# Shifted tile addresses in a three-pass float32 transformer step: gated tiles at three residues, features at a fourth

## The chip, the cores and the metric

The kernel runs on one core of one Trainium2 chip (trn2). The metric is the device time of one execution in microseconds (us); three runs of the kernel before gave a median of 757.47 us, the lowest 757.41 and the highest 758.09. The trace comes from one further execution that took 756.95 us, of which 755.2 us lie between the first and the last instruction (the span). Engines are named as in the profile: PE is the matmul engine, PEld its weight loads, DVE, ACT and POOL the vector, activation and general engines, SP the queue that issues most transfers.

## The reference

One layer of a diffusion backbone over 512 latent tokens and 128 context tokens, 640 in all, width 1024, everything in float32:

```python
h = _rms(x, norm_mix) * (1 + sc1) + sh1          # modulated features
proj = h @ w_in                                  # q, k, v, gb, gc, u
attn = _block_attention(q_r, k_all, v_all)
y_conv = gb * _short_conv(gc * u, conv_w)
merged = jnp.concatenate([_rms(attn, ...), _rms(y_conv, ...)], axis=-1)
x = x + g1 * (merged @ w_out)
h2 = _rms(x, norm_ffn) * (1 + sc2) + sh2
gate, up = jnp.split(h2 @ w_gate_up, 2, axis=-1)
x = x + g2 * ((jax.nn.silu(gate) * up) @ w_down)
```

The context tokens go through the same layer with their own modulation. Nothing in the change touches what is computed.

## The kernel before

**Splits.** A float32 operand is held as two tiles of the type float32r, a rounded high part and the remainder. `split` (lines 150 to 152) makes them: ACT copies the high part, DVE subtracts it. A product is then three matmuls, `mm3` (lines 154 to 157): high by high, high by low, low by high. In `pe.matmul(out, lhsT, rhs)` the second argument is loaded into the array as weights (128 columns of 4 bytes, 512 bytes in each partition) and the third streams past it (the moving operand, 256, 320 or 512 columns). The weight load of a matmul is issued while the matmul ahead of it streams, so at any moment PE reads two places of a partition: the moving operand of one matmul and the weights of the next.

**Which tiles meet.** `wh` and `wl` are the splits of a weight matrix and live in pool A for the whole program. What they meet, in order of time:

- q and k/v: features `hH`, `hL` (modulated, normed x) are loaded, `wh`, `wl` stream: 512 columns for q, 256 for k and v.
- the convolution branch, `conv_mm` (lines 703 to 716), in pieces between the steps of the attention: `wh`, `wl` are loaded, `hH`, `hL` stream with 320 columns.
- the attention itself: KA, KB, VS, qT, ph, pl, none of them beside `wh`.
- the output projection: the mixed features `mx` are loaded (for the last latent block `sx`, for the attention half of the context `m0`, printed as `m` by the profile), `wh`, `wl` of w_out stream with 512 columns.
- gate and up: a scheme with seven products on halves; operands made from w_gate_up are loaded from `wh`, `wl`; the token halves B11, B12, B21, B22 and their sums T1 to T4 stream with 320 columns.
- down: the gated features `gT` (silu(gate) times up, split) are loaded, `wh`, `wl` of w_down stream with 512 columns (256 in the last part). Groups of six, six, five and five of 22 feature blocks; two blocks share one `gT` tile.

**Addresses.** Tiles are placed by pools that are stacked from the left and the right end of each partition, so the size of an early tile shifts all later ones on its side. Two tiles that nothing reads serve for that: `placeA` at the end of pool A on the left (line 601) and `placeF` first on the right (line 170), of PLACE = 48 and 72 floats, 192 and 288 bytes. Slices that are loaded start at whole multiples of 512 bytes in their tile, and moving slices at multiples of 256, so a tile's address modulo 512 tells that of its slices up to 256.

**The ring of gated tiles.** The tag `gT` has GB = 3 buffers of 10,240 bytes in pool GT. It first holds the two tiles of `h2` (line 985), then B12 (line 1045, in `b_tile`), then the gated pairs (line 1183, in `ff_out`). A new tile takes the buffer that the scheduler finds free first.

**Order.** PE runs in program order throughout (`manual_schedule`), and so does DVE around the first products of the feed-forward part; elsewhere the tile layer orders ACT and DVE by priority.

Of the kernel before, what the change touches and what calls it, by code (L numbers as in the profile page):

```python
# [9 lines left out]
F32 = mybir.dt.float32  # L10
F32R = mybir.dt.float32r
# [4 lines left out]
P = 128  # L16
# [4 lines left out]
TOK = NT * P  # L21
# [7 lines left out]
HALF = TOK // 2  # L29
# [21 lines left out]
GB = 3  # L51
# [29 lines left out]
QTB = 3  # L81
WFB = 3
WHB = 4
PLACE = 48, 72
AHEAD = 3
OSQ = 2
AFB = 4
# [4 lines left out]
def build(ctx, tc, x_prompt, x_sample, c, cache_k, cache_v, c_ctx, norm_mix, norm_ffn, w_ada, b_ada,  # L92
# [8 lines left out]
    def open_pool(name, side, names):  # L101
        g = tc.tile_pool(name=name, bufs=1, side=side, reuse_waits="tile")
        pools[name] = (g, g.__enter__())
        for n in names.split():
            where[n] = name
# [7 lines left out]
    def close_pool(name):  # L113
        pools[name][0].__exit__(None, None, None)
# [5 lines left out]
    def T(tag, shape, dt=F32, bufs=1):  # L120
        seq[0] += 1
        return pools[where.get(tag, "A")][1].tile(list(shape), dt, tag=tag, bufs=bufs, name=f"{tag}_{seq[0]}")

    def PB(shape=(P, 512), dt=F32, tag="t"):
        seq[0] += 1
        if kept.get(tag):
            w = kept[tag].pop()
            n = 1
            for y in shape[1:]:
                n *= y  # L130
            w = w[:, :n] if tag != "s" else w
            if tag != "s" and len(shape) > 2:
                names = "abc"[:len(shape) - 1]
                w = w.rearrange("p (" + " ".join(names) + ") -> p " + " ".join(names), **dict(zip(names, shape[1:])))
            return w
        return pools["psum"][1].tile(list(shape), dt, tag=tag, bufs=pbufs[tag], name=f"p{tag}_{seq[0]}")
# [4 lines left out]
    def T2(shape, dt=F32):  # L141
        return T("t2", shape, dt, 2)
# [4 lines left out]
    def early(n):  # L147
        return tc.high_priority(n)

    def split(hi, lo, src):  # L150
        act.activation(hi, src, AF.Copy)  # L151
        dve.tensor_tensor(lo, src, f32(hi), ALU.subtract)  # L152
# [6 lines left out]
    def rstd_of(ss, n, scale, by=1.0, tag="rs"):  # L159

        w = ss.shape[1]
        ms = T("ms", (P, w), F32, 4)
        dve.tensor_scalar(ms, ss, scale * by, EPS * by, ALU.mult, ALU.add)
        r = T(tag, (P, w), F32, {"rB": 1, "rs": 6}.get(tag, NT))
        pool.tensor_tensor(r, ms, neghalf[:, :w], ALU.pow)
        return r

    open_pool("A", "left", "")
    open_pool("F", "right", "placeF of y oz ysum m0 g1 rs5 cp")
    T("placeF", (P, PLACE[1]))  # L170
    open_pool("H", "right", " ".join(f"hH{k} hL{k}" for k in range(KD)))
# [428 lines left out]
    close_pool("B0")  # L600
    T("placeA", (P, PLACE[0]))
    open_pool("B2", "left", "vt KA KB VS qT pr ph pl osq c25 aw es")
# [359 lines left out]
    for x in SEQ.split():  # L962
        if "." in x:
            n, i = (int(y) for y in x[1:].split("."))
# [11 lines left out]
        for _ in range(1):  # L976
            kept[x] = [PS2() if x == "s" else PB(tag=x)]
    open_pool("X", "left", "x2 x2n g2 sx")
    open_pool("GT", "left", "gT")
    open_pool("Y1", "left", "B11 B21")  # L980
    open_pool("D", "right", "mix mx aacc bb")
    phase[0] = 2


    h2 = [T("gT", (P, 4, TOK), F32, GB) for _ in range(2)]
    LO, HI = slice(0, HALF), slice(HALF, TOK)
    x2 = [None] * NT
    x2n = {}
# [53 lines left out]
    B = {}  # L1042

    def b_tile(name):
        w = T("gT" if name == "B12" else name, (P, 2, 4, HALF), F32R, GB if name == "B12" else 1)
        B[name] = [(w[:, 0, i], w[:, 1, i]) for i in range(4)] + [w]

    def quarter(name, part):
# [3 lines left out]
    def b_put(name, src, part):  # L1052
        if name not in B:
            b_tile(name)
        w = B[name][4]
        if name in BHD:
            dve.tensor_copy(w[:, 0, :, part], src)
        else:
            act.activation(w[:, 0, :, part], src, AF.Copy)
        dve.tensor_tensor(w[:, 1, :, part], src, f32(w[:, 0, :, part]), ALU.subtract)  # L1060
# [17 lines left out]
    for j in range(2):  # L1078
        cols = slice(j * 512, (j + 1) * 512)
        for n, t in enumerate(TORD):  # L1080
# [33 lines left out]
            with early(XP[j]):  # L1114
                m = T("mix", (P, 512), F32, 2)
# [6 lines left out]
                else:  # L1122
# [3 lines left out]
                    m = T("mix", (P, 512), F32, 2)  # L1126
# [25 lines left out]
    gT, st, pair = {}, {}, [None]  # L1152
# [9 lines left out]
    def plain(f, bs, toks, mid=None):  # L1162

        ps = [FB(), FB()]
        for x, a in zip(ps, ("A1", "A2")):
            for i in (1, 2):
                if mid is not None and (a, i) == ("A2", 2):
                    mid()
                prod(x, f, f"{a}{i}", bs[i - 1], i == 1, i == 2)
        if toks is LO:  # L1170
            st[f] = T("cg", (P, TOK), F32, 2), T("cu", (P, TOK), F32, 2)
        cg, cu = st[f]
        act.activation(cg[:, toks], ps[0][:, :HALF], AF.Silu)
        dve.tensor_tensor(cu[:, toks], ps[1][:, :HALF], cg[:, toks], ALU.mult)
        if toks is HI:
            ff_out(f, cu)
            del st[f]

    def ff_out(f, cu):
        grp = next(g for g in GROUPS if f in g)  # L1180
        i = (f - grp[0]) % 2
        if i == 0:
            pair[0] = T("gT", (P, 2, 2, TOK), F32R, GB)
        gT[f] = (pair[0][:, i, 0], pair[0][:, i, 1])
        with early(GSP):
            split(gT[f][0], gT[f][1], cu)
# [41 lines left out]
    def ff_end(f):  # L1228
        cg, cu, b3, u2 = st.pop(f)
        dve.tensor_tensor(cg[:, HI], b3[:, :HALF], u2, ALU.add)  # L1230
        act.activation(cg[:, HI], cg[:, HI], AF.Silu)
        dve.tensor_tensor(cu[:, HI], cu[:, HI], cg[:, HI], ALU.mult)
        ff_out(f, cu)
# [78 lines left out]


tile_hymba = with_exitstack(build)

_INS = ["x_prompt", "x_sample", "c", "cache_k", "cache_v", "c_ctx", "norm_mix", "norm_ffn", "w_ada", "b_ada",
# [44 lines left out]
```

## Time and profile before

| what | value |
|---|---|
| median of three runs | 757.47 us |
| profiled execution, whole | 756.95 us |
| its span | 755.2 us |
| PE busy in the span | 737.5 us, 4618 matmuls |
| DVE, ACT, POOL busy | 551.7, 378.8, 42.6 us |
| granted PE clock, mean | 0.999 |

In the rows of a view an instruction stands with its engine, its line, its operation, the tile written and those read, the shape, how many, the busy time and the mean of one in ns. For a matmul "ph<-wh,mx" names the output and both inputs, not which of them moves. Matmuls are pipelined: one of 512 columns is listed with some 389 ns, yet the next starts some 227 ns after it, so the cost of a matmul in a row of them is read from the starts, not from the duration.

### The profile page before, as it was taken

How to read it: one execution, taken by the hardware profiler on the slowest of the kernel's cores; microseconds unless marked ns; L12 is line 12 of the kernel's file. 1: busy time of each engine (PE TensorE's matmuls, PEld its weight loads, DVE VectorE, ACT ScalarE, POOL GpSimd, SP SyncE). 2: the span in 40 equal slices, each digit the busy share in tenths (PEclk: the TensorE clock that was granted, in tenths of full speed). 3: DMA queues.
4: the chain of work that ended last, by engine and by line, in shares of the span. 5: the costliest groups of instructions: out<-in, count | busy, mean ns of one | idle time of the engine just before them, and what ended most of it. 6: DMA issues, size and time to landing. Idle time of an engine off the chain costs nothing.

```text
span 755.2 us, 11953 instructions
## 1 busy us (share of the span) xinstructions
PE 737.5 (98%) x4618; PEld 665.2 (88%) x4618; DVE 551.7 (73%) x997; ACT 378.8 (50%) x745; POOL 42.6 (6%) x75
## 2 busy tenths in 40 slices
PE   7999899999999999999999999999999999999997
PEld 5678888988998887899998799998889998899986
DVE  5558877666666798779979778884678866788653
ACT  5356777667656534765552235553125541255410
POOL 2403101011000110100000000000000000000000
PEclk9999999999999999999999999999999999999999
DMA  9985133532432464031235313133113232222312
GB/s 290 294 236 163 51 104 102 165 92 91 159 107 91 133 224 138 1 112 54 81 118 157 108 58 110 58 111 112 56 56 104 67 112 78 62 86 84 112 56 83
DMA packets 101389, 84.52 MB, mean 112 GB/s; under 512 B 3502, under 2 KB 81650, under 8 KB 101332
## 3 DMA queue, kind: packets, MB, share of 16 engines
q1 hardware_dynamic: 100980, 83.39, 35.9%
q8 instruction: 36, 0.59, 0.3%
q0 software_dynamic: 352, 0.37, 0.3%
q14 instruction: 21, 0.17, 0.1%
HBM read 79.68 MB, written 2.75 MB: 109 GB/s over the span
## 4 chain that ended last, share of the span: by engine, by line
PE 83%; DVE 7%; ACT 5%; DMA 2%; issue 1%; SPq 1%; POOL 0%; ACTq 0%
PE pf L155 17%; PE pf L157 17%; PE pf L156 17%; PE pc L710 3%; PE pc L712 3%; PE pc L711 3%; PE po L868 3%; PE ps L824 2%; PE ph L155 2%; PE ph L157 2%; PE ph L156 2%; PE pc L388 2%; PE pt L851 2%; DMA wf<-in_w_in_dram 1%; PE ps L155 1%
## 5 line engine op out<-in xcount | busy, mean ns | idle before, releaser
L151 ACT ACTIVATE wh<-wf 128x512 fp32r<-128x512 f32 (+1 forms) x68 | 55.5, 816 | 81.1 <-PE pf L157 59.3
L155 PE MATMUL pf<-wh,gT 128*128 128x512 f32 (+1 forms) x225 | 86.9, 386 | 0.0
L156 PE MATMUL pf<-wl,gT 128*128 128x512 f32 (+1 forms) x225 | 86.5, 385 | 0.0
L157 PE MATMUL pf<-wh,gT 128*128 128x512 f32 (+1 forms) x225 | 86.5, 384 | 0.0
L710 PE MATMUL pc<-hH,wh 128*128 128x320 f32 x192 | 61.1, 318 | 0.0
L712 PE MATMUL pc<-hH,wl 128*128 128x320 f32 x192 | 59.3, 309 | 0.0
L711 PE MATMUL pc<-hL,wh 128*128 128x320 f32 x192 | 59.3, 309 | 0.0
L152 DVE TENSOR_TENSOR wl<-wf,wh 128x1024 fp32r<-128x1024 f32 (+1 forms) x34 | 39.4, 1160 | 25.2 <-ACT wh L151 22.1
L155 PE MATMUL pf<-T,wh 128*128 128x320 f32 x160 | 49.6, 310 | 0.5 <-ACT u L1191 0.5
L156 PEld LDWEIGHTS pf<-wl,gT 128*128 128x128 f32 x225 | 42.3, 188 | 8.6 <-issue 0.2
L155 PEld LDWEIGHTS pf<-wh,gT 128*128 128x128 f32 x225 | 42.3, 188 | 8.6 <-issue 0.2
L157 PEld LDWEIGHTS pf<-wh,gT 128*128 128x128 f32 x225 | 42.3, 188 | 8.3
L156 PE MATMUL pf<-T,wh 128*128 128x320 f32 x160 | 49.4, 309 | 0.0
L155 PE MATMUL pf<-T,wl 128*128 128x320 f32 x160 | 49.4, 309 | 0.0
L156 PE MATMUL pf<-T,wl 128*128 128x320 f32 x160 | 49.4, 309 | 0.0
L157 PE MATMUL pf<-T,wl 128*128 128x320 f32 x160 | 49.4, 309 | 0.0
L157 PE MATMUL pf<-T,wh 128*128 128x320 f32 x160 | 49.4, 309 | 0.0
L155 PE MATMUL pf<-B,wl 128*128 128x320 f32 x152 | 47.1, 310 | 0.0
L157 PE MATMUL pf<-B,wl 128*128 128x320 f32 x152 | 47.0, 309 | 0.0
L156 PE MATMUL pf<-B,wl 128*128 128x320 f32 x152 | 47.0, 309 | 0.0
L155 PE MATMUL pf<-B,wh 128*128 128x320 f32 x136 | 42.2, 310 | 1.5 <-DVE cu L1220 1.5
L151 ACT ACTIVATE wl<-wf 128x512 fp32r<-128x512 f32 x34 | 21.2, 625 | 41.6 <-PE pf L156 34.8
(306 smaller groups left out, 2058.7 us busy)
## 6 DMA issues: line engine op xcount, KB each, us to landing
wf<-in_w_gate_up_dram SPq DMA_DIRECT2D x44, 512.0 KB, 4.0
aw<-in_w_ada_dram SPq DMA_DIRECT2D x24, 512.0 KB, 4.1
wf<-in_w_down_dram SPq DMA_DIRECT2D x20, 512.0 KB, 3.3
wf<-in_w_in_dram SPq DMA_DIRECT2D x18, 512.0 KB, 5.5
af<-in_w_ada_dram SPq DMA_DIRECT2D x32, 256.0 KB, 6.4
x<-in_x_sample_dram SPq DMA_DIRECT2D x8, 512.0 KB, 6.2
wf<-in_w_out_dram SPq DMA_DIRECT2D x8, 512.0 KB, 4.4
wf<-in_w_ada_dram SPq DMA_DIRECT2D x8, 512.0 KB, 3.7
```

Source lines behind the costliest of these rows:

```text
L151: act.activation(hi, src, AF.Copy)
L152: dve.tensor_tensor(lo, src, f32(hi), ALU.subtract)
L155: pe.matmul(out, lh, rh, start=start, stop=False, skip_group_check=more)
L156: pe.matmul(out, lh, rl, start=False, stop=False, skip_group_check=more)
L157: pe.matmul(out, ll, rh, start=False, stop=stop, skip_group_check=more)
L388: pe.matmul(out[CG * g:CG * (g + 1)], cp[:, k], w, start=(k < 4), stop=(k >= KD - 4), skip_group_check=True)
L710: pe.matmul(acc, wh[:, k], hH[k][:, c0:c0 + n], start=(k == 0), stop=False)
L711: pe.matmul(acc, wh[:, k], hL[k][:, c0:c0 + n], start=False, stop=False)
L712: pe.matmul(acc, wl[:, k], hH[k][:, c0:c0 + n], start=False, stop=(k == KD - 1))
L824: pe.matmul(s2[:, g, :320], q, kk[:, v, P + g * 320:P + (g + 1) * 320], start=(i == 0), stop=(i == 1))
L851: pe.transpose(tp[:, i, h], u[3][h][:, kt * P:(kt + 1) * P], ident)
L868: pe.matmul(ov, w, x[:, i].rearrange("p a q -> p (a q)"), start=(g == 0 and i == 0 and n == 0), stop=(last and i == len(kts) - 1 and n == 1))
```

## The change

PLACE becomes 64 and 64 floats. The ring `gT` is replaced by three tags `gT0`, `gT1`, `gT2` with one buffer each, padded by 16, 32 and 0 floats, and a function `GT` that hands them out strictly in turn:

```diff
-PLACE = 48, 72
+PLACE = 64, 64
+GPAD = 16, 32, 0
...
+    ring = [-1]
+
+    def GT(shape, dt):
+
+        i = ring[0] = (ring[0] + 1) % GB
+        m = 1
+        for y in shape[1:]:
+            m *= y
+        names = "abc"[:len(shape) - 1]
+        w = T(f"gT{i}", (P, m + GPAD[i]), dt)[:, :m]
+        return w.rearrange("p (" + " ".join(names) + ") -> p " + " ".join(names), **dict(zip(names, shape[1:])))
...
-    open_pool("GT", "left", "gT")
+    open_pool("GT", "left", "gT0 gT1 gT2")
...
-    h2 = [T("gT", (P, 4, TOK), F32, GB) for _ in range(2)]
+    h2 = [GT((P, 4, TOK), F32) for _ in range(2)]
...
-        w = T("gT" if name == "B12" else name, (P, 2, 4, HALF), F32R, GB if name == "B12" else 1)
+        w = GT((P, 2, 4, HALF), F32R) if name == "B12" else T(name, (P, 2, 4, HALF), F32R)
...
-            pair[0] = T("gT", (P, 2, 2, TOK), F32R, GB)
+            pair[0] = GT((P, 2, 2, TOK), F32R)
```

The built programs place the tiles so (address in the partition modulo 512 bytes):

| tiles | before | changed |
|---|---|---|
| `wh`, `wl` | 128 | 128 |
| `hH`, `hL`, `mx` | 128 | 160 |
| `sx`, and KA, KB, VS, qT, ph, pl, pr | 128 | 192 |
| gated tiles | 128 | 192, 256, 384 in turn |
| B11, B21, B22, T1 to T4 | 128 | 384 |
| `m0` | 480 | 480 |

From that follows, for each float32r matmul of 256 columns or more, the distance between its moving operand and the weights loaded behind it (moving minus weights, modulo 512), with the number of matmuls for which it holds:

| part | columns | matmuls | before | changed |
|---|---|---|---|---|
| down, first gated tile of the ring | 512 (256) | 230 (11) | 0 | 448 |
| down, second | 512 (256) | 234 (12) | 0 | 384 |
| down, third | 512 (256) | 177 (6) | 0 | 256 |
| output projection, `mx` | 512 | 186 | 0 | 480 |
| output projection, `sx` | 512 | 24 | 0 | 448 |
| output projection, `m0` | 512 | 23 | 160 | 160 |
| q | 512 | 107 | 0 | 480 |
| k and v | 256 | 116 | 0 | 480 |
| convolution branch | 320 | 521 | 0 or 256 | 32 or 288 |
| gate and up, B and T (B12 among them) | 320 | 1867 | 0 or 256 | 0 or 256 |
| inside the attention | 256 to 512 | some 270 | 0 or 256 | 0 or 256 |

Some hundred more at the seams between parts change their distance too. PE has the same instructions in the same order. On DVE and ACT a few instructions change places where the feed-forward part begins, because the first gated pair (blocks 0 and 1) now takes the buffer of the first `h2` tile, in turn, where it took that of B12. DVE there, before (gT_3260 and gT_3261 are the two `h2` tiles, gT_4125 the first gated pair, T_852 and T_854 the sums T3 and T4, wh and wl operands of gate and up, cu the product up times silu(gate)):

```order
L1073 TENSOR_TENSOR tr_4064<-gT_3261,gT_3260 128x4x128
L152 TENSOR_TENSOR gT_4125<-cu_3963,gT_4125 128x640
L1060 TENSOR_TENSOR T_852_3982<-tr_4064,T_852_3982 128x4x128
L1073 TENSOR_TENSOR tr_4068<-gT_3261,tr_4060 128x4x128
L152 TENSOR_TENSOR wh_4150<-sx_3997,wh_4150 128x512
L206 TENSOR_TENSOR sx_3997<-wf_3990,sx_3997 128x512
L1060 TENSOR_TENSOR T_854_3987<-tr_4068,T_854_3987 128x4x128
L1174 TENSOR_TENSOR cu_4053<-pf_4129,cg_4052 128x320
```

and the same place in the changed kernel, whose line numbers are 13 higher:

```order
L1086 TENSOR_TENSOR tr_4064<-gT_711_3261,gT_710_3260 128x4x128
L165 TENSOR_TENSOR wh_4150<-sx_3997,wh_4150 128x512
L219 TENSOR_TENSOR sx_3997<-wf_3990,sx_3997 128x512
L1073 TENSOR_TENSOR T_852_3982<-tr_4064,T_852_3982 128x4x128
L1086 TENSOR_TENSOR tr_4068<-gT_711_3261,tr_4060 128x4x128
L165 TENSOR_TENSOR gT_870_4125<-cu_3963,gT_870_4125 128x640
L1073 TENSOR_TENSOR T_854_3987<-tr_4068,T_854_3987 128x4x128
L165 TENSOR_TENSOR wh_4181<-sx_3997,wh_4181 128x512
```

The low part of the first gated block (written to gT_4125, in the change gT_870_4125) now stands four places later, behind two steps on the operands wh_4150 and sx_3997 and behind T3 and the subtraction for T4; the set of instructions is the same. A little later DVE has, before, up to the addition for the first seven-product block's `up` (L1220, cu_4295):

```order
L206 TENSOR_TENSOR sx_4224<-wf_4203 128x512
L1204 TENSOR_TENSOR cg_4220<-pf_4259,p_883_4221 128x320
L206 TENSOR_TENSOR sx_4224<-sx_4224,wf_4201 128x512
L152 TENSOR_TENSOR wh_4226<-sx_4224,wh_4226 128x512
L152 TENSOR_TENSOR wh_4260<-wf_4201,wh_4260 128x512
L206 TENSOR_TENSOR sx_4224<-wf_4201,wf_4203 128x512
L152 TENSOR_TENSOR wl_4242<-sx_4224,wl_4242 128x512
L1220 TENSOR_TENSOR cu_4295<-pf_4223,u_892_4293 128x320
```

and in the change:

```order
L219 TENSOR_TENSOR sx_4224<-wf_4203 128x512
L165 TENSOR_TENSOR gT_870_4125<-cu_4053,gT_870_4125 128x640
L165 TENSOR_TENSOR wh_4226<-sx_4224,wh_4226 128x512
L219 TENSOR_TENSOR sx_4224<-sx_4224,wf_4201 128x512
L165 TENSOR_TENSOR wh_4260<-wf_4201,wh_4260 128x512
L1217 TENSOR_TENSOR cg_4220<-pf_4259,p_883_4221 128x320
L165 TENSOR_TENSOR wl_4242<-sx_4224,wl_4242 128x512
L219 TENSOR_TENSOR sx_4224<-wf_4201,wf_4203 128x512
L1233 TENSOR_TENSOR cu_4295<-pf_4223,u_892_4293 128x320
```

The second gated split now stands behind the first operand sum and `cg` three places later; ahead of cu_4295 stands the same set of work as before, counted from the first of these two places.

## The prediction

> **What bounds the kernel now.** First the shares of busy time and the granted clock on the page of the profile, then the chain that ended last:
>
> ```profile
> PE 737.5 (98%) x4618; PEld 665.2 (88%) x4618; DVE 551.7 (73%) x997; ACT 378.8 (50%) x745; POOL 42.6 (6%) x75
> PEclk9999999999999999999999999999999999999999
> PE 83%; DVE 7%; ACT 5%; DMA 2%; issue 1%; SPq 1%; POOL 0%; ACTq 0%
> ```
>
> PE is the bound, at an undisturbed clock, and 83% of the chain is PE itself. So whatever a matmul gains or loses in an unbroken row of them reaches the end almost whole. The stretches (start and first products; attention with the convolution; output projection; start of the feed-forward part; its rest) confirm it:
>
> ```profile
> 17.00:59.00 42.00, 40.76 (x266) 27.94 (x267) 25.07 (x60) 19.22 (x28) 8.72 (x18) 1.00 1.01 271
> 59.00:257.70 198.70, 192.89 (x1401) 173.92 (x1400) 138.10 (x301) 136.88 (x305) 19.96 (x34) 1.00 0.36 112
> 257.70:319.60 61.90, 61.90 (x296) 51.05 (x294) 53.15 (x87) 33.33 (x76) 8.07 (x8) 1.00 0.37 122
> 360.00:755.20 395.20, 389.71 (x2299) 362.74 (x2297) 291.74 (x470) 154.48 (x274) 0.00 (x0) 1.00 0.29 89
> ```
>
> PE (the second number behind the window) fills the output projection fully, the attention to 97%, the rest of the feed-forward part to 99%. There is little idle time in which a longer matmul could hide.
>
> Next, how long a matmul takes in such a row, read from the starts in the timeline of PE. Four stretches at distance 0 or 256 (the moving operand's address minus that of the weights loaded behind it, modulo 512):
>
> ```profile
> 61.09 0.28 PE L156 MATMUL pc<-wl,hH 128*128 128x256 f32 x1
> 62.53 0.28 PE L156 MATMUL pc<-wl,hH 128*128 128x256 f32 x1
> ...
> 203.46 0.31 PE L710 MATMUL pc<-hH,wh 128*128 128x320 f32 x1
> 204.64 0.31 PE L712 MATMUL pc<-hH,wl 128*128 128x320 f32 x1
> ...
> 372.08 0.31 PE L155 MATMUL pf<-T,wl 128*128 128x320 f32 x1
> 373.40 0.31 PE L155 MATMUL pf<-T,wl 128*128 128x320 f32 x1
> ...
> 408.61 0.39 PE L157 MATMUL pf<-wh,gT 128*128 128x512 f32 x1
> 411.78 0.39 PE L156 MATMUL pf<-wl,gT 128*128 128x512 f32 x1
> ```
>
> Between the first and the second row of each pair lie 12 steps of k and v (1.44 us, 120 ns each), 8 of the convolution (1.18 us, 147 ns), 9 of gate and up (1.32 us, 147 ns) and 14 of down (3.17 us, 226 ns; 227 below). From 256 to 512 columns the step grows by 107 ns, 0.417 ns a column; 120 less 256 times that leaves 13.3 ns that do not depend on the columns. A weight load (128 columns each time) runs beside each matmul, so part of these 13 ns may be its doing.
>
> Distance 0 is not the whole of it, since the trace has one place at another. The context block's attention half in the output projection, `m0`, lies at 160:
>
> ```profile
> 285.27 0.39 PE L155 MATMUL ph<-wh,sx 128*128 128x512 f32 x1
> 288.00 0.39 PE L155 MATMUL ph<-wh,m 128*128 128x512 f32 x1
> 290.81 0.40 PE L155 MATMUL ph<-wh,mx 128*128 128x512 f32 x1
> ...
> L155 PE MATMUL ph<-wh,m x8: 392/398/400, 257.7 to 290.1; 128*128 128x512 f32 x8
> L156 PE MATMUL ph<-wl,m x8: 392/394/400, 257.9 to 290.3; 128*128 128x512 f32 x8
> L157 PE MATMUL ph<-wh,m x8: 390/397/400, 258.2 to 290.6; 128*128 128x512 f32 x8
> L156 PE MATMUL ph<-wl,mx x64: 387/389/398, 260.8 to 316.6; 128*128 128x512 f32 x64
> L155 PE MATMUL ph<-wh,sx x8: 389/389/389, 285.3 to 319.1; 128*128 128x512 f32 x8
> ```
>
> Twelve matmuls on `sx` (distance 0) take 2.73 us, 227 ns each; the twelve on `m0` right behind them, with the same columns, 2.81 us, 234 ns each. The durations (least, median, most of each line) agree: 389 without spread at 0, 390 to 400 at 160. The same happened at 257.7, and the clock in that stretch is 1.00. So here a distance that is no multiple of 256 costs some 7 ns a matmul; taken from the durations and their spread, 1 to 11.
>
> **The change part by part.** It moves the addresses of the modulated, mixed and gated features and nothing of the work. The 1,867 matmuls of gate and up keep 0 or 256, those inside the attention too. I take 7.2 ns (0.08 us over twelve are 6.7 ns; 234.2 against the 226.4 of down are 7.8; this is the middle) for each 512-column matmul that leaves the multiples of 256.
>
> *Down.* The first and the second ring tile go to 448 and 384: 464 matmuls of 512 columns, 23 of 256. 487 times 7.2 ns is 3.5 us. The third goes to 256 and costs nothing, as the convolution shows, which has both 0 and 256 and one step time. Their rows today are at the floor:
>
> ```profile
> L155 PE MATMUL pf<-wh,gT 128*128 128x512 f32 (+1 forms) x225 | 86.9, 386 | 0.0
> L156 PE MATMUL pf<-wl,gT 128*128 128x512 f32 (+1 forms) x225 | 86.5, 385 | 0.0
> L157 PE MATMUL pf<-wh,gT 128*128 128x512 f32 (+1 forms) x225 | 86.5, 384 | 0.0
> L156 PE MATMUL ph<-wl,mx 128*128 128x512 f32 x64 | 25.0, 390 | 0.0
> L156 PE MATMUL ps<-wl,hH 128*128 128x512 f32 x32 | 12.7, 396 | 0.4 <-DVE wl L536 0.4
> ```
>
> (The means of down lie under 389 because ten of each line have 256 columns.)
>
> *Output projection.* 186 matmuls on `mx` go to 480. Their mean is 390, 1 ns above the floor already, so I add 6.2 ns: 1.2 us. 24 on `sx` go to 448: 0.2 us. Together 1.3 us. The operands wait for nothing else there, PE is full.
>
> *q.* 107 matmuls go to 480; at a mean of 396 they already pay 7 ns of unrest between waits for loads. I add 0.1 us.
>
> *k, v and the convolution.* 116 matmuls of 256 columns and 521 of 320 leave the multiples of 256, and the trace has no steady row of such widths elsewhere. From above they are bounded by what 512 columns show, 400 against 389, 11 ns; from below by the shortest in the attention, which come right behind a pause:
>
> ```profile
> L868 PE MATMUL po<-ph,VS x80: 278/283/385, 102.7 to 257.4; 128*128 128x256 f32 x80
> L824 PE MATMUL ps<-KB,qT x64: 302/309/312, 91.0 to 240.6; 128*128 128x320 f32 x64
> ```
>
> 5 ns under the median at 256 columns, 7 under it at 320. So -7 to +11, and I take 3.6, half of the 512-column price, as these come in short rows between other work: 637 times 3.6 ns is 2.3 us.
>
> *Order.* The first gated split moves behind some steps of the operands. That is the stretch before the longest wait of the feed-forward part:
>
> ```profile
> PE pf L155 <- DVE cu L1220: 1.5, 1, 1.5
> 362.65 0.48 DVE L1220 TENSOR_TENSOR cu<-pf,u 128x320 f32<-128x320 f32 x1
> 363.19 0.41 PE L155 MATMUL pf<-B,wh 128*128 128x320 f32 x1 [1.48 <-DVE cu L1220]
> ```
>
> DVE has the same set of work ahead of that addition before and after, so I put it at 0; one DVE step of 0.7 us more or less could fall ahead of it, so -0.7 to +0.7. Behind the addition PE's S4 product of that block waits, and all that follows. The gated pair itself is needed only by down, which the rows above show at 408.
>
> The sum: 3.5 + 1.3 + 0.1 + 2.3 = 7.2 us. Onto the profiled execution's own 756.95 us (span 755.2, the 1.75 around it unchanged) that makes 764.1; the median of the runs shown is 757.47, 0.5 higher, and the forecast stays with the sum. The ends: with +11 ns everywhere (674 + 139 + 521 = 1,334 matmuls) and +0.7, 772; with -2 ns on the 512-column ones (387 against 389), -7 and -5 on the others and -0.7, 750.5.
>
> **The rivals.** *A shorter period.* If addresses repeat every 128 bytes, 384 is as good as 0, the second ring tile keeps its time and 1.8 us fall away: 762.3. For it: 0 and 256 are alike, so the period is under 512. Against: nothing tells 128 from 256. It ends on the same side.
>
> *Distance does nothing.* `m0` may be slow for its own sake, and only 24 matmuls say otherwise; then the forecast is the time before, 757, with the order as the one open term. Against it: `m0` and `sx` differ in nothing else, and the price comes and goes within one or two matmuls. [...]
>
> *Faster.* 0 may be a mediocre distance. 13.3 ns of each step do not depend on the columns, and the matmuls that start behind a pause are up to 7 ns shorter than in the steady row, so a state exists in which the load disturbs less. If 32 and 480 hold the convolution, k and v in it, 521 times 7 and 139 times 5 ns are 4.3 us, and 2 ns on the 674 others 1.3: 751.3. It decides as soon as the narrow matmuls save more than the 4.8 us that the forecast adds in down and the output projection, or as these stay at their floor. Against: the one other distance that the trace shows is worse, and its shortest matmul, 390, is still above the floor.
>
> **How the numbers follow.** Forecast 64%, the shorter period 12%, both slower; nothing 10%; faster 14%. A difference of 0.2%, 1.5 us, is about what a measurement of this kernel can tell from none. So slower 0.76, same 0.10, faster 0.14. The forecast's own range, with 4 to 11 ns on the 697 matmuls of down and the output projection (2.8 to 7.7 us) and 0 to 7 on the 637 narrow ones (0 to 4.5), is 760 to 769; to leave no more than 2 in 10 outside, the range reaches to 754 below and 769 above.
>
> **What would show it.** Right: the median duration of `gT` matmuls at 512 columns splits by ring tile, some 396 for two of them and 389 for the third; `mx` goes from 389 to some 396; the convolution's rows L711 and L712 from 309 to 311 to 316; gate and up stay at 309; the wait at L1220 (now L1233) stays near 1.5 us; granted clock 1.00. Wrong: `mx` or `gT` at 389 throughout (distance does nothing), or below it (faster); convolution rows near 302 would mean that the narrow term has the wrong sign; `gT` slow in one tile alone would be the shorter period.

## The result, and the profile after

| | before | changed |
|---|---|---|
| median of three runs | 757.47 us | 764.06 us (763.80 to 764.28) |
| ratio of the medians, 95% interval | | 1.0084 [1.0061, 1.0107] |
| profiled execution, its span | 755.2 us | 762.0 us |

The changed kernel is slower by 6.6 us, and its time is the predicted one to a tenth of a microsecond. The steps behind the forecast are less good than that: two of them failed, in opposite directions, so the agreement to a tenth is luck.

First the engines' shares and the chain that ended last, on the page of the changed kernel:

```profile
PE 743.7 (98%) x4618; PEld 667.4 (88%) x4618; DVE 552.3 (72%) x997; ACT 378.6 (50%) x745; POOL 42.6 (6%) x75
PE 83%; DVE 7%; ACT 4%; DMA 3%; issue 1%; SPq 1%; POOL 0%; ACTq 0%
```

PE is busy for 6.2 us longer with the same 4618 matmuls, so the matmuls themselves became longer. The groups that the prediction named, with the mean of one in ns behind the busy time, and the views of single tiles (least, median and most in ns):

```profile
L168 PE MATMUL pf<-wh,gT 128*128 128x512 f32 (+1 forms) x225 | 88.2, 392 | 0.0
L169 PE MATMUL pf<-wl,gT 128*128 128x512 f32 (+1 forms) x225 | 87.4, 388 | 0.0
L170 PE MATMUL pf<-wh,gT 128*128 128x512 f32 (+1 forms) x225 | 87.7, 390 | 0.0
...
L169 PE MATMUL ph<-wl,mx x64: 392/396/398, 261.7 to 318.6; 128*128 128x512 f32 x64
L168 PE MATMUL ph<-wh,sx x8: 393/396/399, 286.8 to 321.2; 128*128 128x512 f32 x8
...
L724 PE MATMUL pc<-hL,wh x192: 305/309/314, 73.5 to 256.0; 128*128 128x320 f32 x192
L725 PE MATMUL pc<-hH,wl x192: 304/309/314, 73.6 to 256.2; 128*128 128x320 f32 x192
```

Down rose from 386, 385, 384 to 392, 388, 390, `mx` and `sx` from 389 to 396, as forecast. The convolution's rows did not: 309 before and after, with a wider spread. The cost of one matmul is again read from the starts. For each half of the output columns a group of down begins with 30 matmuls on its first gated pair (two feature blocks, five token blocks, three matmuls each); then the second and the third pair take turns by token block, six matmuls each (three for a third pair of one feature block). The first two rows are of the kernel before, the last two of the changed one, each pair 27 steps apart in such an unbroken row of 30:

```profile
539.19 0.39 PE L155 MATMUL pf<-wh,gT 128*128 128x512 f32 x1
545.31 0.39 PE L155 MATMUL pf<-wh,gT 128*128 128x512 f32 x1
```

```profile
544.05 0.40 PE L168 MATMUL pf<-wh,gT 128*128 128x512 f32 x1
550.35 0.39 PE L168 MATMUL pf<-wh,gT 128*128 128x512 f32 x1
```

6.12 us are 226.7 ns a step at distance 0, 6.30 us are 233.3 ns at 448. By ring tile, over all 512-column matmuls of down, the mean distance from the start of the matmul ahead is 233.2 ns for the first (448), 232.6 for the second (384) and 229.4 for the third (256), against 226.9 before.

One thing in the trace was in nobody's list. Where the feed-forward part begins, PE waits for the addition `cu` (L1233) as before, and then runs at half speed for a while. In the timeline of the changed kernel:

```profile
363.19 0.31 PE L170 MATMUL pf<-T,wl 128*128 128x320 f32 x1
365.25 0.41 PE L168 MATMUL pf<-B,wh 128*128 128x320 f32 x1 [1.75 <-DVE cu L1233]
...
365.83 0.47 PE L168 MATMUL pf<-B,wh 128*128 128x320 f32 x1
369.04 0.36 PE L168 MATMUL pf<-B,wl 128*128 128x320 f32 x1
```

Between the last two rows lie 12 steps of 267 ns, where these matmuls take 147 ns elsewhere. The windows (PE busy is the second number behind the window, the granted clock the third from the end) show the clock itself, for the two stretches of 3.41 us before and after 365.73:

```profile
362.32:365.73 3.41, 1.66 (x12) 1.40 (x11) 3.41 (x8) 2.46 (x5) 0.00 (x0) 1.00 0.01 2
365.73:369.14 3.41, 3.41 (x15) 3.41 (x14) 2.07 (x5) 0.62 (x2) 0.00 (x0) 0.50 0.54 158
```

Before, the wait there was 1.48 us, now it is 1.75. The order on DVE sets it: four traces with the strict turn (this one, and below ring_only, after_again and after_third) have 1.75, four with the old order (the kernel before, narrow_32, order_kept, order_kept_2) 1.46 to 1.48. DVE is busy for the whole 3.41 us of the first window, and in its order the second gated split (0.82 us) now lies nearer to the addition; that this one instruction makes the difference was not tested. The longer wait by itself costs next to nothing here, because a shorter wait ahead of it changed as well (PE's idle time stands in the brackets). The first row is of the kernel before, the second of the changed one:

```profile
357.93 0.41 PE L155 MATMUL pf<-T,wh 128*128 128x320 f32 x1 [0.52 <-ACT u L1191]
356.20 0.42 PE L168 MATMUL pf<-T,wh 128*128 128x320 f32 x1 [0.43 <-ACT p L1204]
```

At the end of the output projection PE runs 2.03 us later than in the kernel before, and right behind the addition 2.06 us later. The 1.54 us more that follow are those of the half clock.

Matched instruction by instruction, the 6.8 us between the two spans lie so: down 3.2, output projection 1.0, the start of the feed-forward part 1.6, q with k, v and the convolution 0.1. The last 0.8 arose near 227 us in the attention; the profiles of ring_only, narrow_32 and order_kept below have 1.0 to 1.2 us more at the same place, early_before has 0.1, and of these ring_only, narrow_32 and early_before change no address that is used there, so this is a difference between executions and not the change.

### The profile page after: what moved, and what is told of

It is laid out like the page before. It is cut to its first block, busy times and chain, and to the rows that moved or that the text cites. A ratio compares the mean times of both kernels' runs of the same rounds, so it can differ in the third digit from the quotient of the medians.

```text
span 762.0 us, 11956 instructions
## 1 busy us (share of the span) xinstructions
PE 743.7 (98%) x4618; PEld 667.4 (88%) x4618; DVE 552.3 (72%) x997; ACT 378.6 (50%) x745; POOL 42.6 (6%) x75
## 4 chain that ended last, share of the span: by engine, by line
PE 83%; DVE 7%; ACT 4%; DMA 3%; issue 1%; SPq 1%; POOL 0%; ACTq 0%
PE pf L168 17%; PE pf L170 17%; PE pf L169 17%; PE pc L723 3%; PE pc L725 3%; PE pc L724 3%; PE ph L168 2%; PE ph L170 2%; PE ph L169 2%; PE po L881 2%; PE ps L837 2%; PE pc L401 2%; PE pt L864 2%; DMA wf<-in_w_in_dram 1%; PE ps L168 1%
## 5 line engine op out<-in xcount | busy, mean ns | idle before, releaser
L168 PE MATMUL pf<-wh,gT 128*128 128x512 f32 (+1 forms) x225 | 88.2, 392 | 0.0
L170 PE MATMUL pf<-wh,gT 128*128 128x512 f32 (+1 forms) x225 | 87.7, 390 | 0.0
L724 PE MATMUL pc<-hL,wh 128*128 128x320 f32 x192 | 59.4, 309 | 0.0
L725 PE MATMUL pc<-hH,wl 128*128 128x320 f32 x192 | 59.3, 309 | 0.0
L1283 DVE TENSOR_TENSOR dm<-pf,g 128x512 f32<-128x512 f32 (+1 forms) x41 | 27.7, 676 | 22.7 <-PE pf L170 22.5
```

Source lines behind the costliest of these rows:

```text
L168: pe.matmul(out, lh, rh, start=start, stop=False, skip_group_check=more)
L170: pe.matmul(out, ll, rh, start=False, stop=stop, skip_group_check=more)
L724: pe.matmul(acc, wh[:, k], hL[k][:, c0:c0 + n], start=False, stop=False)
L725: pe.matmul(acc, wl[:, k], hH[k][:, c0:c0 + n], start=False, stop=(k == KD - 1))
L1283: dve.tensor_tensor(dm, ps[:, :n], g2[cc][:, oc], ALU.mult)
```

## Experiments

**The order alone: ring_only.** The three tags in strict turn, on the addresses of before. It separates the order of the buffers from the distances.

```diff
+GPAD = 0, 0, 0
...
+    def GT(shape, dt):
...
-    open_pool("GT", "left", "gT")
+    open_pool("GT", "left", "gT0 gT1 gT2")
```

> All addresses as before (distances 0 and 256 only), but gated tiles handed out strictly in turn as in the change: the order on DVE and ACT of the change alone. If only distances cost: the time of before, 757.5 us. If the order costs what the change's trace shows at the start of the feed-forward part: 1.6 us more, 759.1, of which most is a window of some 3.4 us at half the granted clock behind the wait at L1233; without that window at most 0.3 us more.

Measured: 759.09 us, ratio 1.0011 [1.0002, 1.0019] over 758.11. The eleven executions fall into two kinds by their mean granted clock: five at 0.999 or 1.000 with a median of 758.11, the time before, and six at 0.998 or 0.997 with 759.35. A stretch of 3.41 us at half clock lowers the mean over 757 us by 0.002, which is what the six show. So the strict turn costs nothing on these addresses but a chance of half clock.

**The features alone: right_only.** Only the place of the modulated and mixed features is moved, to 480.

```diff
-PLACE = 48, 72
+PLACE = 48, 64
```

> Only placeF goes from 72 to 64 floats: hH, hL and mx move by 32 bytes, gated tiles and the order stay. On-record prices: output projection 1.2, q 0.1, k, v and convolution 2.3, together 3.6, 761.1 us. If narrow matmuls (256 and 320 columns) are immune, as the change's trace suggests: 1.0 for mx and 0.1 to 0.3 for q, 758.7 us; mx at some 233 ns from start to start, convolution at 147.

Measured: 759.07 us, ratio 1.0014 [1.0006, 1.0023]. The rows of the output projection and the convolution:

```profile
L156 PE MATMUL ph<-wl,mx x64: 392/395/396, 262.7 to 319.6; 128*128 128x512 f32 x64
...
L711 PE MATMUL pc<-hL,wh x192: 306/309/312, 74.3 to 257.0; 128*128 128x320 f32 x192
L712 PE MATMUL pc<-hH,wl x192: 305/309/313, 74.4 to 257.2; 128*128 128x320 f32 x192
```

The 512-column matmuls on `mx` took 232.9 ns from start to start, 1.0 us in all over the trace before. The 320-column ones at 32 and 288 took 146.8 to 147.1 ns, as before. The 256-column ones of k and v took 118.3 ns at 480, which is 1.5 ns less than the 119.8 at 0. The same twelve steps that the prediction read at 120 ns (1.44 us) take 1.42 us in the changed kernel:

```profile
61.07 0.28 PE L169 MATMUL pc<-wl,hH 128*128 128x256 f32 x1
62.49 0.28 PE L169 MATMUL pc<-wl,hH 128*128 128x256 f32 x1
```

The traces of after_again, after_third and order_kept have 118.3 to 118.4 ns there too, those of ring_only and narrow_32, with k and v at 0, have 119.8. The difference in time, 0.96 us, is what the wide matmuls give: the forecast's 2.3 us for the narrow ones are not there.

**Narrow matmuls, many of them: narrow_32.** The kernel before with B11 and what follows it moved by 32 bytes, so that some 1,800 matmuls of gate and up run at 32 or 288.

```diff
-    open_pool("Y1", "left", "B11 B21")
+    open_pool("Y1", "left", "padB B11 B21")
+    T("padB", (P, 8))
```

> Before, with B11, B21, B22 and T1 to T4 moved by 32 bytes: 1819 matmuls of 320 columns in long steady rows go from 0 or 256 to 32 or 288, nothing else. If narrow matmuls are immune: 757.5 us, 147 ns from start to start. At the on-record 3.6 ns each: 6.5 us more, 764; at the wide price of 7.2: 770.6.

Measured: 757.70 us, ratio 0.9996 [0.9987, 1.0005]. The timeline, nine steps apart:

```profile
372.69 0.31 PE L155 MATMUL pf<-T,wl 128*128 128x320 f32 x1
374.01 0.31 PE L155 MATMUL pf<-T,wl 128*128 128x320 f32 x1
```

1.32 us, 147 ns a step, as in the kernel before. At 3.6 ns each, 1,800 matmuls would have cost 6.5 us. At 320 columns the distances 32 and 288 cost nothing here that can be measured.

**The addresses with the order of before: order_kept and, again, order_kept_2.** All addresses of the change, but each tile takes the buffer that it had before, so DVE's order is the old one too.

```diff
-        i = ring[0] = (ring[0] + 1) % GB
+        ring[0] += 1
+        i = ring[0] if ring[0] < GB else (2, 0, 1)[ring[0] % GB]
```

> The change's addresses with the order of before (the first gated pair takes B12's buffer again). Distances of down: 234 matmuls of 512 columns at 448, 177 at 384, 230 at 256. If the order costs 1.6 us in the change: 764.1 - 1.6, and 0.3 less for 53 fewer matmuls off 256, 762.2 us, and no half-clock window. If it costs nothing: 763.8 us.

> The change's addresses with the order of before, beside the change on the same chip: all executions at a mean clock of 0.999 or 1.0, some 3.6 us over the kernel before. The strict order is worth the difference to the next run: 0.3 for the matmuls, and 0.5 to 0.9 on average for half-clock windows; more than that would be a cost of the order by itself.

Measured: 761.74 us, ratio 1.0049 [1.0036, 1.0062], and 761.23, ratio 1.0045 [1.0032, 1.0057]; in twelve executions the mean clock is never under 0.999. From order_kept_2, the wait at the addition (engine, tile and line, what it waited for: us in total, how often, the longest) and 27 steps of the gated tile that now comes first in a group:

```profile
PE pf L169 <- DVE cu L1234: 1.5, 1, 1.5
...
542.44 0.39 PE L169 MATMUL pf<-wh,gT 128*128 128x512 f32 x1
548.56 0.39 PE L169 MATMUL pf<-wh,gT 128*128 128x512 f32 x1
```

The wait is the old one. The order also decides down: here the tile at 256 is first in its group, so its rows run unbroken, 6.12 us for 27 steps, 226.7 ns, the floor. It holds 234 wide matmuls, and the two costly tiles share the rest, while the change gives 177 to the tile at 256 and lets it take turns with the one at 384. Over all of down that is 2.3 us above the time before, against 3.2 in the change.

**The change twice more: after_again, after_third.** The changed kernel without an edit, timed again beside the kernel before.

> The change once more, for more executions beside order_kept's and ring_only's. If the strict order adds only a half-clock window in some executions: the executions fall in two groups, mean granted clock 0.997 to 0.998 in about half of them, and these some 1.3 us longer than those at 0.999 to 1.0; those at full clock stand where order_kept stands, plus 0.3 for 53 more matmuls off 256, some 4 us over the kernel before. If the order costs by itself, those at full clock stand 1 us or more higher than that.

> The change itself: about half of the executions at a mean clock of 0.997 to 0.998 and some 0.9 to 1.3 us longer than the others; those at full clock 0.3 us over order_kept_2 if the order costs nothing by itself, 1 us or more over it if it does.

Measured: 763.27 us, ratio 1.0066 [1.0054, 1.0079], with a mean clock of 0.998 in three of six; and 763.68, ratio 1.0072 [1.0059, 1.0086], 0.998 or less in two of five. Counting the first three runs, the seven executions at 0.998 or less have a median of 763.80, the seven others of 762.98. Half clock is thus worth about 0.8 us of the 5 to 6.6 us that the change costs, in half of its executions.

The two profiles tell when it comes. The clock record of the change starts with full clock at 7.33 us, and its half stretch begins at 365.73 and lasts 3.41 us: the full stretch ahead of it lasts 358.40 us, 105 times 3.413, the one behind it 392.53 us, 115 times. In the kernel before the full stretch runs from 6.71 us for 747.52 us, 219 times 3.413. So in these two records the clock changes on a grid of 3.413 us, and the grid lies elsewhere from execution to execution: the half stretch of after_again begins at 366.73 us. The windows on that grid that hold the wait, first after_again, then after_third, and the kernel before:

```profile
363.32:366.73 3.41, 1.66 (x12) 1.40 (x11) 3.41 (x8) 2.04 (x5) 0.00 (x0) 1.00 0.01 2
366.73:370.14 3.41, 3.41 (x15) 3.41 (x14) 2.62 (x6) 1.15 (x2) 0.00 (x0) 0.50 0.72 200
```

```profile
362.24:365.65 3.41, 3.19 (x22) 2.93 (x20) 3.38 (x7) 2.24 (x5) 0.00 (x0) 1.00 0.01 2
365.65:369.06 3.41, 1.87 (x13) 1.87 (x14) 3.41 (x7) 1.37 (x3) 0.00 (x0) 1.00 0.03 8
```

```profile
361.70:365.11 3.41, 1.93 (x14) 1.92 (x14) 3.41 (x7) 1.11 (x3) 0.00 (x0) 1.00 0.00 0
365.11:368.52 3.41, 3.41 (x25) 3.41 (x24) 2.53 (x6) 2.06 (x4) 0.00 (x0) 1.00 0.87 243
```

In after_again, as in the first profile of the change, the wait of 1.75 us lies whole in one window; PE is busy there for 1.66 of 3.41 us, and the next window runs at half clock. In after_third the same wait straddles an edge; the emptier window still has 1.87 us, and nothing follows. The profile of ring_only, with the same wait across an edge (2.09 us busy), had none either. The wait of the kernel before, 1.48 us, lies whole in a window and leaves 1.93 us busy: no half clock. By an estimate from these two lengths, with every phase equally likely, a wait of 1.75 us falls whole into a window in (3.41 - 1.75) / 3.41 = 49% of the executions; 13 of the 25 executions of the change and of ring_only have a mean clock of 0.998 or less, 2 of 56 of the kernel before and 0 of 12 of order_kept (only the profiles tell where the half stretch lay). In after and after_again 1.75 us of idleness in one window were enough.

**The wait taken out: early_before, early_after.** The addition is given a higher priority for the first seven-product block, so that DVE does it ahead of two operand steps; in the kernel before and in the change.

```diff
-        dve.tensor_tensor(cu[:, HI], b3[:, :HALF], u3, ALU.add)
+        with early(60 if f == NPLAIN else 0):
+            dve.tensor_tensor(cu[:, HI], b3[:, :HALF], u3, ALU.add)
```

> The kernel before, with the addition that PE waits for at the start of the feed-forward part (L1220, for the first seven-product block) put two steps earlier on DVE by priority. If the wait is what DVE has ahead of it: about 1.3 us less, 756.9 beside some 758.2, PE idle there under 0.5 us. If something else is late next (the operand of the same product): no change.

> The change with the same addition two steps earlier. If the idle time of PE before it brings the half-clock windows: none at that place, all executions in one group, some 1.2 us below the change's executions at full clock and 2.2 below those at half clock, so near 761.5. If the windows come by chance anywhere: some executions at a mean clock of 0.997 to 0.998 as before.

Measured: early_before 756.82 us, ratio 0.9988 [0.9979, 0.9996]; early_after 761.76, ratio 1.0055 [1.0043, 1.0067]. No execution of either is under 0.999 in its mean clock. In the timeline of early_before, and then of early_after, PE's first matmul behind the wait:

```profile
362.09 0.41 PE L155 MATMUL pf<-B,wh 128*128 128x320 f32 x1 [0.27 <-DVE cu L1221]
```

```profile
365.54 0.42 PE L168 MATMUL pf<-B,wh 128*128 128x320 f32 x1 [0.66 <-DVE cu L1234]
```

The wait shrinks to 0.27 and 0.66 us. early_before is the fastest kernel of the study, 0.76 us under the kernel before: in its trace 1.3 us are gained at the wait, and 0.4 given back by 395 us. In the change the step brings 1.9 us against after_third, wait and half clock together. early_after against early_before shows what the change costs without half clock, as neither meets it: 4.9 us. In their traces the distances give 4.4 of them, and the smaller gain at the start of the feed-forward part (0.7 us in early_after, 1.3 in early_before) the rest.

**Other distances: sweep_a, sweep_fine.** The order of before, the gated tiles at 352, 320 and 288 (sweep_a); at 508, 240 and 0, that is 4 and 16 bytes off a multiple of 256, and one control (sweep_fine). One execution each.

```diff
+GPAD = 8, 8, 8
...
+    open_pool("GT", "left", "padG gT0 gT1 gT2")
+    T("padG", (P, 40))
```

```diff
+GPAD = 64, 64, 0
+GOFF = 1, 4, 0
...
+        w = T(f"gT{i}", (P, m + GPAD[i]), dt)[:, GOFF[i]:GOFF[i] + m]
```

> Order and everything else of before, gated tiles at 352 (234 matmuls of 512 columns), 288 (230) and 320 (177), that is 96, 32 and 64 modulo 256. If every distance off the multiples of 256 costs alike: 232 to 234 ns from start to start for all three, 641 times 6 ns, 3.8 us over before. If addresses repeat every 128 bytes and sign does not matter, nothing new either. If some distance is better than 0: under 226 ns for one of them.

> As before, but the first ring tile 4 bytes and the second 16 bytes further (distances 508 and 240, the latter 16 under 256), the third at 0; the tiles are read from such an offset. If only the place within a line of 32 bytes or more counted: 227 ns for all three. If any shift counts: 231 to 234 ns at 4 and 16 bytes, 2.6 us over before.

Measured: 761.82 and 759.53 us, beside a median of 758.18 for the kernel before; down alone is 3.5 and 2.3 us longer. In the timeline of sweep_a 27 unbroken steps of the tile at 288, and in that of sweep_fine 30 steps in which the tiles at 508 and 240 take turns:

```profile
541.93 0.40 PE L170 MATMUL pf<-wh,gT 128*128 128x512 f32 x1
548.23 0.40 PE L170 MATMUL pf<-wh,gT 128*128 128x512 f32 x1
```

```profile
526.46 0.39 PE L170 MATMUL pf<-wh,gT 128*128 128x512 f32 x1
533.41 0.40 PE L170 MATMUL pf<-wh,gT 128*128 128x512 f32 x1
```

233.3 ns at 288, and 231.7 ns at 508 and 240: four bytes are enough. All distances of the study for 512 columns, as mean distance from the start of the matmul ahead over a tile's matmuls (59 to 78 on each of the three lines; `mx` 186 in all). Where tiles take turns, up to 1 ns can belong to the neighbour:

| distance | ns | kernel |
|---|---|---|
| 0 | 226.9; 227.7 | before; sweep_fine |
| 256, rows unbroken | 227.4 | order_kept_2 |
| 256, in turn with 384 | 229.4 | changed |
| 448 | 233.2; 232.8 | changed; order_kept_2 |
| 384 | 232.6; 231.8 | changed; order_kept_2 |
| 480 (`mx`) | 233.0 | changed |
| 352 | 233.4 | sweep_a |
| 320, in turn with 352 | 229.5 | sweep_a |
| 288 | 233.3 | sweep_a |
| 508 | 232.6 | sweep_fine |
| 240 | 231.4 | sweep_fine |

At 512 columns none of these distances is better than 0. Of those off the multiples of 256, all but 320 cost 4.5 to 6.5 ns; 320 costs 2.6, in turn with a tile at 352. That is what 256 costs in turn with 384, so 320 may be as free as 256; no unbroken row of it was run.

**Which weights count: low_apart.** The low halves of two of the three gated tiles are moved 64 bytes away from their high halves, so only the weights of the third matmul of each three change their distance (to 448 and 192).

```diff
+LOFF = 16, 16, 0
...
+        if halves:
+            o = m // 2 + LOFF[i]
+            return [w[:, c:c + m // 2].rearrange("p (a b) -> p a b", b=TOK) for c in (0, o)]
```

> As before, but in two of three ring tiles the low halves lie 64 bytes further than the high halves (distance 448 or 192), high halves at 0 or 256. The low half is loaded while the second of the three matmuls streams (high by low) and used by the third. If the moving operand and the weights being loaded behind it disturb each other: the second matmul of each three (L175) is the longer one, by up to 7 ns, the third is not. If a matmul is slowed by the address of its own weights: the third (L176). If neither, all three share it through the phase: each some 2 ns longer.

Measured: 759.22 us, one execution; down is 1.8 us longer. In the groups of lines, the first, second and third matmul of the three, with their mean:

```profile
L174 PE MATMUL pf<-wh,gT 128*128 128x512 f32 x215 | 84.1, 391 | 0.0
L175 PE MATMUL pf<-wl,gT 128*128 128x512 f32 x215 | 84.1, 391 | 0.0
L176 PE MATMUL pf<-wh,gT 128*128 128x512 f32 x215 | 84.8, 395 | 0.0
```

From each start to the next, in the two moved tiles: 228.3 and 228.4 ns for the first, 228.9 and 229.3 for the second, 235.8 and 235.5 for the third; in the control tile 227.2, 227.7 and 227.6. By the prediction's own definition, the weights loaded behind a matmul, the second should be the long one. It is the third, whose own weights lie apart. A recorded start precedes its step (a duration of 389 ns against a step of 227), so the record may be one matmul early; whether a matmul's own weights count, or the load beside it, stays open. In the change both halves of a tile lie at the same distance from the operands that stream past, so the sum does not depend on it.

## Why the prediction was right, and where it was not

- **PE sets the time, and a longer matmul reaches the end.** Right: 6.2 us more of PE time (half clock among it) in 6.8 us more of span, the same chain.
- **A wide matmul off the multiples of 256 costs 7.2 ns.** Right in kind, a little high: 6.3 ns at 448, 5.7 at 384 in down, some 5.5 at 480 (1.0 us over 186 matmuls). The step "the third goes to 256 and costs nothing" holds only for unbroken rows; in turn with a tile at 384 it cost 2.5 ns, 0.4 us. Down measured 3.2 for 3.5, the output projection 1.0 for 1.3, q 0.1 for 0.1: 4.4 of the 4.9 us forecast.
- **"I take 3.6, half of the 512-column price"** for the 637 narrow matmuls, 2.3 us: this step failed. At 320 columns right_only has their price at 0, narrow_32 with three times as many matmuls confirms it, and the rows L724 and L725 stayed at 309; at 256 columns it is -1.5 ns, 0.2 us in all. The two bounds, -7 and +11, held both between them; half the price of another width was no evidence.
- **"DVE has the same set of work ahead of that addition before and after, so I put it at 0"**: this step failed too, and the bound of 0.7 us with it. For DVE and PE alone the 0 was nearly right: the wait grew by 0.27 us, but PE stands only 0.03 us later behind it. What the step left out is the clock: behind the wait of 1.75 us a 3.41-us stretch at half clock followed in two of four profiles, behind 1.46 to 1.48 us in none of four; it is worth 1.6 us in the profiled execution. By medians it is 0.8 us in the executions of the change that have it and 1.2 in those of ring_only. The forecast expected a granted clock of 1.00 throughout.
- **The sum.** 7.2 us were forecast. The failed terms, 2.3 too much and 1.6 too little, nearly cancel, and 0.8 us in the attention by the chance of the execution closed the rest: luck, not a better sum. The three comparisons of the change gave 6.6, 5.1 and 6.1 us; the terms that the runs support add to 4.4 from the distances and 0.8 to 1.2 from half clock in half of the executions, some 4.9. The rest, 0.2 to 1.7 us, has no cause shown beyond the spread between executions. Two pairs close better: order_kept has 2.3 from down and 1.2 from projection and q, 3.5 in sum, and 3.6 measured both times; early_after lies 4.9 over early_before.
- **The rivals.** The shorter period is refuted: 384 costs as much as 448. That the addresses do nothing is refuted at 512 columns by right_only (232.9 ns at 480) and both sweeps (229.5 to 233.4 ns off the multiples of 256), against 226.9 ns at 0; the rows of 320 columns, at 147 ns throughout, agree with it. Faster is refuted as a forecast: at 512 columns no distance measured was under the 226.9 ns of 0, at 320 the 147 ns did not change, and the 7 ns under the median behind a pause did not come. It holds in small at 256 columns, 1.5 ns where it reckoned with 5. A rival that nobody named is open: the price may hang on the address of the loaded tile alone. In every run at 512 columns the streamed `wh` and `wl` stayed at 128 modulo 512 and only the loaded tile moved, so "a multiple of 256 apart" and "loaded from 128 modulo 256" say the same there.

What stays open: distance or address of the loaded tile; and why the price shows at 512 columns, is 0 at 320 and turns round at 256. At 320 columns the runs that changed the distance moved the streamed tile, at 256 and 512 the loaded one, so width and moved operand are not told apart at 320. One window also stands against the reading of the clock: at the end of early_before, PE is busy for 1.62 of 3.41 us, and the next window was still granted at full clock.

## What to carry to other kernels

Where wide float32r matmuls run in unbroken rows, place the streamed operand and the loaded weights a multiple of 256 bytes apart (here 226.7 ns a step of 512 columns at 0 and at 256, 233.3 at 448 and at 288, with the streamed operand at 128 modulo 512), and give the best-placed buffer to the tile with the most matmuls (in down 2.3 us over the time before in place of 3.2). A price read from one width should not be carried to another (at 448 or 480: 6.3 ns at 512 columns, -1.5 at 256; at 320 columns 0 at 32 and 288): the other width wants a measurement of its own. And a change of order that looks harmless on a busy queue can lengthen the one wait of the matmul engine, here from 1.48 to 1.75 us, so far that a stretch at half clock follows; look at the length of that wait and not only at the set of work ahead of it.

## What the runs showed of the hardware that was not expected

- The time of a 512-column matmul depends on the addresses to 4 bytes: 226.9 ns at 0, 232.6 at 508 (one execution). At 320 columns, where the streamed tile was moved, it did not change (147 ns at 0, 32, 256 and 288). At 256 columns it was shorter at 480: 119.8 ns at 0, 118.3 at 480.
- Half clock came after a window of 3.41 us in which PE had been busy for 1.66 us, and not after 1.87 (after_third), 1.93 (before) or 2.09 us (ring_only), nor after 1.62 us at the end of early_before, the exception named above; in the record of the change the windows lie on a grid from the first full-speed one (365.73 - 7.33 = 358.40 us, 105 times 3.413). Of the waits at the addition those of 1.46 to 1.48 us brought it in none of four profiles, those of 1.75 us in two of four, and it cost 12 steps of 267 in place of 147 ns. right_only had one such window at its start, 1.61 us busy, with half clock behind it.
